# Strided attention outputs kept by residue: one ScalarE copier, a later value step and a later exponential in a fused decoder layer

## The chip, the cores and the metric

The kernel runs on one core of a Trainium2 chip. Time is device microseconds of one execution. A core has a matmul engine (TensorE, PE; its weight loads are PEld), VectorE (DVE), ScalarE (ACT), GpSimd (POOL), and SyncE (SP), which here only issues DMAs. Each engine takes its instructions in the order in which the program lists them; semaphores order the engines among themselves.

## The reference, cut to what matters

One layer of a hybrid decoder in fp32: an input projection, attention with eight heads and a gating unit beside it, an output projection and a SwiGLU network, for 2048 prompt positions and a small sample group. The change touches the prompt's attention alone. Each head evaluates three branches (window, dilation): (128, 1), (512, 4) and (2048, 16). They are merged with weights proportional to their softmax sums:

```python
    s = jnp.einsum('bnqrhc,bnkrhc->bnrhqk', qb, kc).astype(jnp.float32)
    s = s * (HEAD_DIM ** -0.5) + bias[None, None, None]
    s = jnp.where(valid[None, :, None, None], s, NEG_INF)
    lse = jax.nn.logsumexp(s, axis=-1)
    p = jnp.exp(s - lse[..., None])
    o = jnp.einsum('bnrhqk,bnkrhc->bnqrhc', p.astype(vc.dtype), vc)
...
    w = jax.nn.softmax(jnp.stack(lses, axis=0), axis=0)
    return jnp.sum(w[..., None] * jnp.stack(outs, axis=0).astype(jnp.float32), axis=0)
```

## The kernel before, in words

**Stages.** The input projection comes first (to about 610 us), then attention (about 610 to 1000 us), the output projection and the SwiGLU network in three blocks of positions.

**Items and steps.** The first two branches are computed together as a *band*: for each of 16 query blocks of 128 positions, scores against up to five key blocks. The third branch is *strided*: positions with the same residue modulo 16 form a block of 128, four residues make one strided item, so a head has 16 band items and 4 strided items. In heads 1 to 6 the order is `OTHER`: 0, 1, s, 2, 3, 4, 5, s, 6 to 9, s, 10 to 13, s, 14, 15, with s a strided item; so strided items stand at places 2, 7, 12 and 17 of the 20. The first and last heads have other orders.

A small planner, `Plan`, sets the order of the program. `at(step, phase, fn)` records a call; calls run sorted by step, then by phase (`early`, `exp`, `low`, `scores`, `turn`, `mid`, `values`, `out`, `misc`, `store`), then by when they were recorded. One item starts in each step: item i at step x = 240 + i.

- A band item has its scores (L864) at step x and its bias, with a running minimum, on VectorE (L870) at x + 1. The exponential on ScalarE (L875) is at x + 2, and the transposes on TensorE (L891) at x + 3, emptied by ScalarE (L896) and VectorE (L902). Four band items form a group. Behind its last item the group's values (L916) are computed in two parts, at x + 4 and x + 5, into PSUM bank 3, and copied out by ScalarE (L930; for a head's first group L927 and L928) at x + 6, "early".
- For a strided item GpSimd first reorders keys and queries (L937, three casts from every sixteenth position) at x - 2. The scores (L945) are at x, the bias and minimum on VectorE (L950, L952) and GpSimd (L953) at x + 1, the exponential (L956) at x + 3, its row sum (L960) and the transposes (L965, L967) at x + 4. The values (L974) go into the same PSUM bank 3, at the first step from x + 6 on that is not in the set `taken`; `strided_out` copies them out at the next step, "early".

`taken` holds the steps of the band values, so that two groups don't meet in bank 3. Scores go through two PSUM buffers in turn, so that the scores of item x need the bias of item x - 2.

**Outputs of the strided branch.** `o3` holds a head's strided outputs as [channel, i, residue], position 16 i + residue. `strided_out` writes it in two halves of two residues each, ScalarE one (L986), VectorE the other (L984); consecutive elements of one residue lie 64 bytes apart.

**Factors and merge.** When a head's items are done, `Stats` works out a weight for each branch and position: a product (L1002), two small matmuls (L1008), a copy (L1012), `weights_a` (three operations on VectorE, L1018 to L1020, and an exponential on ScalarE, L1021), `weights_b` (L1026 to L1030), and a store to DRAM (L1034). `merge_load` reads the factors back, spread over the partitions, and `merge` combines four pieces of 512 positions in three parts: band output times factor (L1055), strided output times factor (L1057), sum (L1059). GpSimd does this during the next head, one part a step from step 11 to 22, among its other work; in the last head VectorE does the first piece.

Of the kernel before, what the change touches and what calls it, by code (L numbers as in the profile page):

```python
# [10 lines left out]
F32 = mybir.dt.float32  # L11
F32R = mybir.dt.float32r
AF = mybir.ActivationFunctionType
# [6 lines left out]
P = 128  # L20
T = 2048
NT = T // P
# [3 lines left out]
C = 64  # L26
# [38 lines left out]
def hymba_step(ctx: ExitStack, tc: tile.TileContext, A: dict, O: dict):  # L65
    nc = tc.nc
    sync, act, dve, pool, pe = nc.sync, nc.scalar, nc.vector, nc.gpsimd, nc.tensor
# [7 lines left out]
    turn = [0, 0, 0, 0]  # L75
# [87 lines left out]
    rp = right.enter_context(tc.tile_pool(name="rp", bufs=1, side="right"))  # L163
# [480 lines left out]
    B0 = 240  # L644
# [49 lines left out]
    for half in range(2):  # L694
        for ki, kind in enumerate(ORDER[half]):
            for gi, tiles in enumerate(GROUPS):
# [13 lines left out]
                for j, tj in enumerate(tiles):  # L710
                    t = half * 8 + tj
                    e, ph = e0 + 2 * j, "out"
                    if last:
                        e, ph = e0, "early"
# [261 lines left out]
    def strided_out(it):  # L976
        r4, h = it["n"], it["h"]
        if r4 == 0:
            o3s[h] = rp.tile([P, P, NT], F32, name="o3", tag="wide", bufs=2)
        for z in range(2):  # L980
            dst = o3s[h][0:C, :, r4 * 4 + z * 2:r4 * 4 + z * 2 + 2].rearrange("p i r -> p r i")
            src = it["o"][z * C:(z + 1) * C, z * 256:(z + 1) * 256].rearrange("p (r i) -> p r i", r=2)
            if z:
                dve.tensor_copy(dst, src)  # L984
            else:
                act.activation(dst, src, AF.Copy)  # L986

    s12 = {}

# [2 lines left out]
    class Stats:  # L992
# [21 lines left out]
        def weights_a(self):  # L1014

            m3 = self.st["t"][0:self.r1, 2, :]
            self.f = f = self.small("f", 3)
            dve.tensor_tensor(f[:, 2, :], self.s[:, 0, :], m3, op=OP.min)  # L1018
            dve.tensor_sub(f[:, 0, :], f[:, 2, :], self.s[:, 0, :])
            dve.tensor_sub(f[:, 1, :], f[:, 2, :], m3)  # L1020
            act.activation(f[:, 0:2, :], f[:, 0:2, :], AF.Exp)  # L1021

        def weights_b(self):
            f, m = self.f, self.f[:, 2, :]
# [25 lines left out]
    def merge(h, ch, eng, part=None):  # L1050
        f1, f3 = mf[h, ch]
        x = obs[h][:, ch * 512:(ch + 1) * 512]
        y = o3s[h].rearrange("p i r -> p (i r)")[:, ch * 512:(ch + 1) * 512]
        if part in (None, 0):
            eng.tensor_mul(x, x, f1)  # L1055
        if part in (None, 1):
            eng.tensor_mul(y[0:C], y[0:C], f3[0:C])  # L1057
        if part in (None, 2):
            eng.tensor_add(x[0:C], x[0:C], y[0:C])  # L1059

    def merge_store(h, c0, c1):
        for z in range(2):
# [46 lines left out]
    for h in range(H):  # L1109
        r4 = 0  # L1110
        for n in FIRST if h == 0 else LAST if h == H - 1 else OTHER:
            if n == "s":
                items.append(dict(kind="s", h=h, n=r4))
                r4 += 1
                continue
            if n % 4 == 0:
                grp = {}
            items.append(dict(kind="b", h=h, n=n, grp=grp))
            if n % 4 == 3:

                taken.update(B0 + len(items) - 1 + y for y in (4, 5))
    NI = len(OTHER)
    L = B0 + len(items) - 1
    at(222, "misc", begin, 0)
# [13 lines left out]
    def stats_of(h, steps, r0, r1):  # L1138
        d = {}
        at(*steps[0], lambda: d.update(s=Stats(h, sts[h], r0, r1)))  # L1140
        for (y, ph), fn in zip(steps, "a b c weights_a weights_b store".split()):
            at(y, ph, lambda fn=fn: getattr(d["s"], fn)())

    for h in range(H):
# [4 lines left out]
        if end:  # L1149

            x = s0 - NI
            stats_of(h, [(x + y, ph) for y, ph in ((14, "early"), (14, "turn"), (15, "early"), (15, "misc"), (16, "early"), (16, "mid"))], 0, 64)
            steps = ((2, "early"), (2, "turn"), (3, "early"), (4, "early"), (5, "early"), (5, "early"))
            at(x + 18, "mid", merge_load, h, 0)
            at(x + 18, "mid", merge_load, h, 1)
            for part in range(3):
# [1 line left out]
                at(x + 21 + part, "store", merge, h, 1, pool, part)  # L1158
            at(x + 24, "store", merge_store, h, 0, 2)
        else:  # L1160
            steps = ((2, "misc"), (3, "misc"), (4, "early"), (4, "misc"), (5, "misc"), (6, "mid"))

            for ch, (a, b) in enumerate(((8, 11), (8, 14), (14, 17), (20, 24) if ahead else (17, 20))):
                at(s0 + a, "mid", merge_load, h, ch)
# [887 lines left out]
```

## Time and profile before

| what | value |
|---|---|
| median of 3 runs | 2718.59 us (2712.78 to 2735.36) |
| the profiled execution | 2712.56 us, span 2710.8 us |
| busy share of the span | PE 94%, PEld 80%, DVE 51%, ACT 44%, POOL 51% |
| mean granted TensorE clock | 0.962 |

The span runs from the first to the last instruction; an execution's own time is a little longer. A row of instructions in order of time has the start, the busy time, the engine, the line, the operation, output and inputs, and the number of instructions; in brackets how long the engine stood idle before it, and what ended that. A row of a group has the total and the mean duration (in ns) behind the bar, then the idle time before and its causes. A row of waits reads "engine, what it stood before <- what it waited for: us in total, times, longest".

### The profile page before, as it was taken

The page shows a single profiled execution, that of the slowest core. Times are in us where ns is not written, and L with a number is a line of the kernel's source. Part 1 is how long each engine was busy: PE and PEld are TensorE (multiplying, and loading weights), DVE is VectorE, ACT ScalarE, POOL GpSimd, SP SyncE. Part 2 cuts the span into 40 slices and gives each one's busy share as a digit, 9 for nine tenths or more (in the row PEclk, how much of TensorE's full clock was granted, in tenths as well). Part 3 has the DMA queues.
Part 4 walks back from the last instruction along what each step waited for, and adds up shares of the span by engine and source line. Part 5 has one row for each costly group of instructions (what it writes and reads, how often), then busy time and mean ns, then how long its engine had stood idle before and what let it go on. Part 6 is the DMA issues. An engine that isn't in the chain of part 4 may idle for free.

```text
span 2710.8 us, 38610 instructions
## 1 busy us (share of the span) xinstructions
PE 2539.2 (94%) x13578; PEld 2180.0 (80%) x13578; DVE 1380.8 (51%) x2756; ACT 1200.5 (44%) x2537; POOL 1388.1 (51%) x1048
## 2 busy tenths in 40 slices
PE   8998999998888778899999999999999998999997
PEld 6777777776666557899899988899999987999996
DVE  3268784436665753443444455444444456444445
ACT  6423344436565545545445444423232335433333
POOL 1035553224756752767676653535454533666663
PEclk9999999999988889799999999899999998899998
DMA  8765844674555456345555465445454453455553
GB/s 249 215 195 152 260 144 138 183 254 157 173 154 161 116 156 201 117 152 177 169 164 186 136 186 187 133 147 196 154 180 166 170 174 129 162 197 203 198 201 118
DMA packets 298166, 468.46 MB, mean 173 GB/s; under 512 B 26839, under 2 KB 163208, under 8 KB 292084
## 3 DMA queue, kind: packets, MB, share of 16 engines
q1 hardware_dynamic: 283588, 443.31, 50.7%
q10 hardware_dynamic: 14384, 22.68, 3.3%
q8 instruction: 108, 1.77, 0.3%
q14 instruction: 86, 0.70, 0.1%
HBM read 374.38 MB, written 161.64 MB: 198 GB/s over the span
## 4 chain that ended last, share of the span: by engine, by line
PE 49%; POOL 9%; issue 9%; DVE 5%; ACT 5%; DMA 4%; SPq 1%; POOLq 0%; DVEq 0%; ACTq 0%
PE ps_o L1627 11%; PE ps_m L1555 7%; PE ps_m L1554 7%; PE ps_m L1556 7%; POOL op L1497 2%; DMA ab_d<-pair 2%; PE ps_o L916 2%; PE ps_s L864 1%; ACT fr L1465 1%; PE ps_s L945 1%; POOL pair L1477 1%; POOL fr L1480 1%; POOL pair L1486 1%; PE ps_t L891 1%; POOL dw L137 1%
## 5 line engine op out<-in xcount | busy, mean ns | idle before, releaser
L1497 POOL TENSOR_TENSOR op<-fr,op 128x512 fp32r<-128x512 f32 x385 | 488.6, 1298 | 316.6 <-ACT op L1493 299.0
L1554 PE MATMUL ps_m<-xh,op 128*128 128x384 f32 (+4 forms) x1932 | 629.8, 326 | 8.5 <-ACT xh L1431 5.4
L1555 PE MATMUL ps_m<-xl,op 128*128 128x384 f32 (+4 forms) x1932 | 627.8, 325 | 7.1 <-DVE xl L1434 7.1
L1556 PE MATMUL ps_m<-xh,op 128*128 128x384 f32 (+4 forms) x1932 | 627.6, 325 | 0.0
L1627 PE MATMUL ps_o<-dw,hw 128*128 128x512 f32 x2040 | 484.3, 392 | 9.3 <-DVE acc L1629 9.3
L1627 PEld LDWEIGHTS ps_o<-dw,hw 128*128 128x128 f32 x2040 | 379.7, 188 | 91.7 <-DVE acc L1629 15.9
L1554 PEld LDWEIGHTS ps_m<-xh,op 128*128 128x128 f32 x1932 | 377.6, 195 | 13.7 <-ACT xh L1431 6.1
L1555 PEld LDWEIGHTS ps_m<-xl,op 128*128 128x128 f32 x1932 | 378.0, 196 | 11.8 <-DVE xl L1434 7.8
L1556 PEld LDWEIGHTS ps_m<-xh,op 128*128 128x128 f32 x1932 | 377.3, 195 | 0.0
L1629 DVE TENSOR_TENSOR acc<-acc,ps_o 128x512 f32<-128x512 f32 (+1 forms) x362 | 247.0, 686 | 214.1 <-PE ps_o L1627 214.1
L1594 ACT ACTIVATE ps_t<-zn 128x384 f32<-128x384 f32 (+1 forms) x126 | 58.3, 463 | 485.9 <-DVE zn L1577 376.7
L1493 ACT ACTIVATE op<-fr 128x512 fp32r<-128x512 f32 x396 | 235.6, 622 | 16.2 <-DMA fr<-ab_d 13.3
L137 POOL TENSOR_TENSOR dw<-fd,dw 128x1024 fp32r<-128x1024 f32 x66 | 158.6, 2403 | 122.6 <-ACT dw L134 122.5
L317 PE MATMUL ps_s<-wh,xh 128*128 128x512 f32 x480 | 197.4, 411 | 6.5 <-ACT xh L134 6.0
L318 PE MATMUL ps_s<-wl,xh 128*128 128x512 f32 x480 | 191.8, 400 | 1.7 <-DVE wl L225 1.7
L319 PE MATMUL ps_s<-wh,xl 128*128 128x512 f32 x480 | 191.2, 398 | 0.0
L1497 POOL TENSOR_TENSOR op<-pair,op 128x512 fp32r<-128x512 f32 x63 | 81.3, 1299 | 117.0 <-ACT op L1493 117.0
L1604 ACT ACTIVATE hw<-ps_t 128x384 fp32r<-128x384 f32 (+1 forms) x126 | 56.1, 453 | 176.7 <-DVE ps_t L1600 175.7
L317 PEld LDWEIGHTS ps_s<-wh,xh 128*128 128x128 f32 x480 | 92.5, 193 | 36.8 <-issue 8.4
L318 PEld LDWEIGHTS ps_s<-wl,xh 128*128 128x128 f32 x480 | 92.8, 193 | 20.5 <-DVE wl L225 3.2
L603 POOL TENSOR_TENSOR vl<-kv,vh 100x512 fp32r<-100x512 f32 (+1 forms) x32 | 45.5, 1424 | 124.5 <-ACT vh L597 44.4
L319 PEld LDWEIGHTS ps_s<-wh,xl 128*128 128x128 f32 x480 | 92.4, 192 | 20.4 <-DVE xl L137 0.3
(452 smaller groups left out, 4576.6 us busy)
## 6 DMA issues: line engine op xcount, KB each, us to landing
fr<-ab_d SPq DMA_DIRECT2D x308, 256.0 KB
fd<-in_w_down_dram SPq DMA_DIRECT2D x66, 512.0 KB
out_ks_dram<-in_cache_k_dram SPq DMA_DIRECT2D x56, 512.0 KB
out_vs_dram<-in_cache_v_dram SPq DMA_DIRECT2D x56, 512.0 KB
ab_d<-fr SPq DMA_DIRECT2D x88, 256.0 KB
raw<-in_w_in_dram SPq DMA_DIRECT2D x72, 256.0 KB
qk_d<-pair SPq DMA_DIRECT2D x64, 256.0 KB
ab_d<-pair SPq DMA_DIRECT2D x63, 256.0 KB
```

Source lines behind the costliest of these rows:

```text
L137: (eng_lo or pool).tensor_sub(lo, src, hi.bitcast(F32))
L317: pe.matmul(o[j], xh[:, k, :], wh, start=(k == 0), stop=False)
L318: pe.matmul(o[j], xh[:, k, :], wl, start=False, stop=False)
L319: pe.matmul(o[j], xl[:, k, :], wh, start=False, stop=(k == KD - 1))
L1493: act.activation(ops[f, j][0], ab[f][j], AF.Copy)
L1497: (pool if f or j in POOL_LOW else dve).tensor_sub(lo_, ab[f][j], hi.bitcast(F32))
L1554: pe.matmul(out, wh[:, ks], xh[:, :, k], start=(k == 0), stop=False)
L1555: pe.matmul(out, wh[:, ks], xl[:, :, k], start=False, stop=False)
L1556: pe.matmul(out, wl[:, ks], xh[:, :, k], start=False, stop=(k == 3))
L1594: act.activation(g, c, AF.Silu)
L1627: pe.matmul(ps[0:nr], l_, r_[:, cs], start=(z == 0 and y == 0), stop=(z == FC - 1 and y == len(pairs) - 1))
L1629: dve.tensor_add(B.acc[i][0:nr, cs], B.acc[i][0:nr, cs], ps[0:nr])
```

## The change

`o3` is kept as [channel, residue, i], so each residue's 128 positions are contiguous. ScalarE makes both copies of `strided_out`. The merge walks through `o3` with the residue innermost, so that neighbouring elements lie 512 bytes apart: its product with the factor reads and writes that way, its sum reads that way; band output and factors keep their order. `taken` also holds the step of the band copy, x + 6, so strided values move to a later step. The exponential leaves `weights_a`, becomes `weights_e`, and comes a step later, while the rest of `weights_a` comes earlier in its step.

```diff
         if r4 == 0:
-            o3s[h] = rp.tile([P, P, NT], F32, name="o3", tag="wide", bufs=2)
+            o3s[h] = rp.tile([P, NT, P], F32, name="o3", tag="wide", bufs=2)
         for z in range(2):
-            dst = o3s[h][0:C, :, r4 * 4 + z * 2:r4 * 4 + z * 2 + 2].rearrange("p i r -> p r i")
-            src = it["o"][z * C:(z + 1) * C, z * 256:(z + 1) * 256].rearrange("p (r i) -> p r i", r=2)
-            if z:
-                dve.tensor_copy(dst, src)
-            else:
-                act.activation(dst, src, AF.Copy)
+            act.activation(o3s[h][0:C, r4 * 4 + z * 2:r4 * 4 + z * 2 + 2, :],
+                           it["o"][z * C:(z + 1) * C, z * 256:(z + 1) * 256].rearrange("p (r i) -> p r i", r=2), AF.Copy)
...
-            act.activation(f[:, 0:2, :], f[:, 0:2, :], AF.Exp)
+
+        def weights_e(self):
+            act.activation(self.f[:, 0:2, :], self.f[:, 0:2, :], AF.Exp)
...
-        y = o3s[h].rearrange("p i r -> p (i r)")[:, ch * 512:(ch + 1) * 512]
+        y = o3s[h][0:C].rearrange("p r i -> p i r")[:, ch * 32:(ch + 1) * 32, :]
+        by_token = lambda v: v[0:C].rearrange("p (i r) -> p i r", r=NT)
...
-            eng.tensor_mul(y[0:C], y[0:C], f3[0:C])
+            eng.tensor_mul(y, y, by_token(f3))
         if part in (None, 2):
-            eng.tensor_add(x[0:C], x[0:C], y[0:C])
+            eng.tensor_add(by_token(x), by_token(x), y)
...
-                taken.update(B0 + len(items) - 1 + y for y in (4, 5))
+                taken.update(B0 + len(items) - 1 + y for y in (4, 5, 6))
...
-        for (y, ph), fn in zip(steps, "a b c weights_a weights_b store".split()):
+        for (y, ph), fn in zip(steps, "a b c weights_a weights_e weights_b store".split()):
...
-            stats_of(h, [(x + y, ph) for y, ph in ((14, "early"), (14, "turn"), (15, "early"), (15, "misc"), (16, "early"), (16, "mid"))], 0, 64)
-            steps = ((2, "early"), (2, "turn"), (3, "early"), (4, "early"), (5, "early"), (5, "early"))
+            stats_of(h, [(x + y, ph) for y, ph in ((14, "early"), (14, "turn"), (15, "early"), (15, "misc"), (16, "early"), (16, "early"), (16, "mid"))], 0, 64)
+            steps = ((2, "early"), (2, "turn"), (3, "early"), (4, "early"), (4, "early"), (5, "early"), (5, "early"))
...
-            steps = ((2, "misc"), (3, "misc"), (4, "early"), (4, "misc"), (5, "misc"), (6, "mid"))
+            steps = ((2, "misc"), (3, "misc"), (4, "early"), (4, "early"), (5, "early"), (5, "misc"), (6, "mid"))
```

How this moves instructions, at three places. On TensorE, around a strided item's values in a middle head (`ps_o` and `ps_t` are PSUM banks, `eT` the transposed exponentials, `sq` the reordered operands), the rows before were:

```order
L864 MATMUL ps_s<-k,ql 128x256
L974 MATMUL ps_o_6494<-eT,v 64x128 x4
L864 MATMUL ps_s<-k,qh 128x384
L864 MATMUL ps_s<-k,qh 128x256
L864 MATMUL ps_s<-k,ql 128x384
L864 MATMUL ps_s<-k,ql 128x256
L965 MATMUL ps_t_6515<-ident,e_6437 128x128 x4
L891 MATMUL ps_o_6522<-ident,e 128x128 x3
L891 MATMUL ps_t_6527<-ident,e 128x128 x2
L945 MATMUL ps_s<-sq 128x128 x8
```

The same place with the change:

```order
L864 MATMUL ps_s<-k,ql 128x256
L864 MATMUL ps_s<-k,qh 128x384
L864 MATMUL ps_s<-k,qh 128x256
L864 MATMUL ps_s<-k,ql 128x384
L864 MATMUL ps_s<-k,ql 128x256
L965 MATMUL ps_t_6507<-ident,e_6437 128x128 x4
L891 MATMUL ps_o_6514<-ident,e 128x128 x3
L891 MATMUL ps_t_6519<-ident,e 128x128 x2
L974 MATMUL ps_o_6522<-eT,v 64x128 x4
L945 MATMUL ps_s<-sq 128x128 x8
```

The four value matmuls went behind the next scores and transposes, and now stand right ahead of the strided scores.

On VectorE, where a head's factors are made (`s` holds the copied sums, `f` the factors, the L870 rows are band biases of the next head), the rows before were:

```order
L1012 COPY s_5874<-ps_o_5871 128x32
L870 ISA e,st<-ps_s,b 128x384
L870 ISA st 128x1
L1018 TENSOR_TENSOR f<-s_5874,st 128x16
L1019 TENSOR_TENSOR f<-f,s_5874 128x16
L1020 TENSOR_TENSOR f<-f,st 128x16
L870 ISA e,st<-ps_s,b 128x512
L870 ISA st 128x1
L1026 TENSOR_TENSOR dd<-f,s_5874 128x16
```

With the change (the lines of the file moved up by four there):

```order
L1008 COPY s_5874<-ps_o_5871 128x32
L1014 TENSOR_TENSOR f<-s_5874,st 128x16
L1015 TENSOR_TENSOR f<-f,s_5874 128x16
L1016 TENSOR_TENSOR f<-f,st 128x16
L870 ISA e,st<-ps_s,b 128x384
L870 ISA st 128x1
L870 ISA e,st<-ps_s,b 128x512
L870 ISA st 128x1
L1024 TENSOR_TENSOR dd<-f,s_5874 128x16
```

The three small operations went ahead of one band bias.

On ScalarE, behind a band group's copy (here a head's first group), the rows before were:

```order
L928 ACTIVATE ob<-ps_o_5981 64x384
L956 ACTIVATE e_5959<-e_5959 128x512
L875 ACTIVATE e,st<-e,st 128x640
L986 ACTIVATE o_6027<-ps_o_6016 64x2x128
L875 ACTIVATE e,st<-e,st 128x640
L967 ACTIVATE eT<-ps_t_6039 128x512
```

With the change:

```order
L928 ACTIVATE ob<-ps_o_5981 64x384
L956 ACTIVATE e_5959<-e_5959 128x512
L875 ACTIVATE e,st<-e,st 128x640 x2
L967 ACTIVATE eT<-ps_t_6031 128x512
L896 ACTIVATE pt<-ps_t_6038 128x3x128
L981 ACTIVATE o_6052<-ps_o_6046 64x256 x2
```

The strided copy, now two of them, went behind one band exponential and the copies of the transposes, and stands a step later.

## The prediction

> **What bounds the kernel now.** I read busy time by stretch, since the change touches only the attention stage, about 610 to 1000 us. The first row below is the whole stage, the second six whole heads of it; the columns are the busy time of PE, PEld, DVE, ACT and POOL, the granted clock, and the DMA share. The last two come from a finer cut of the same view.
>
> ```profile
> 610.00:1000.00 390.00, 324.51 (x2134) 236.22 (x2131) 249.87 (x573) 226.67 (x529) 248.64 (x227) 0.91 0.51 150
> 640.00:925.00 285.00, 240.05 (x1617) 177.79 (x1616) 178.80 (x430) 170.28 (x400) 183.56 (x171) 0.92 0.54 160
> ...
> 762.00:765.00 3.00, 1.30 (x12) 1.33 (x13) 2.61 (x7) 1.96 (x6) 1.86 (x2) 1.00 0.02 9
> 765.00:768.00 3.00, 3.00 (x15) 2.38 (x14) 2.19 (x5) 1.79 (x4) 0.73 (x1) 0.54 0.00 0
> ```
>
> In the six heads TensorE works 240 of 285 us; the 45 us in which it stands still are what this change can win, and no other engine is busy more than 65%. So the stage is a chain of waits, not a full engine. The clock adds to it: right behind a stretch in which TensorE worked 1.30 of 3 us, the granted clock is 0.54; over the six heads it averages 0.92, so another 8%, 23 us, goes to slow clock.
>
> Next the waits. The first four rows are TensorE's own in those six heads; the last two are of other engines, over the whole stage.
>
> ```profile
> PE ps_s L945 <- DVE st L870: 23.3, 17, 1.8
> PE ps_o L974 <- ACT ob L930: 10.6, 10, 1.8
> PE ps_s L945 <- POOL ob L1059: 2.9, 2, 1.5
> ...
> PE ps_o L974 <- ACT ob L928: 2.5, 6, 0.4
> ...
> DVE o L984 <- ACT o L986: 60.0, 30, 3.5
> ...
> ACT f L1021 <- DVE f L1020: 24.7, 9, 7.1
> ```
>
> TensorE waits before the strided scores (L945) for a late band bias on VectorE (L870), and before the strided values (L974) for ScalarE's copy out of the same PSUM bank (L930, L928). Behind the first stands the fifth row: VectorE's half of the strided copy (L984) waits for ScalarE's half (L986) in 30 of 32 cases, 2 us each, although the two write different elements. They interleave in one tile. Behind the second stands in part the last row, ScalarE standing before the exponential of the factors.
>
> One head is enough to see the pattern, because every later one repeats it:
>
> ```profile
> 726.25 1.08 PE L945 MATMUL ps_s<-sq 128*128 128x128 f32 x8 [1.45 <-DVE st L870]
> 735.10 0.66 PE L974 MATMUL ps_o<-eT,v 128*64 128x128 f32 x8 [0.33 <-ACT ob L930]
> 738.49 1.08 PE L945 MATMUL ps_s<-sq 128*128 128x128 f32 x8 [1.29 <-DVE st L870]
> 746.95 0.66 PE L974 MATMUL ps_o<-eT,v 128*64 128x128 f32 x8 [1.78 <-ACT ob L930]
> 750.64 1.94 PE L945 MATMUL ps_s<-sq 128*128 128x128 f32 x8 [0.66 <-DVE st L870]
> 759.45 0.66 PE L974 MATMUL ps_o<-eT,v 128*64 128x128 f32 x8 [0.42 <-ACT ob L928]
> 763.70 1.08 PE L945 MATMUL ps_s<-sq 128*128 128x128 f32 x8 [1.81 <-DVE st L870]
> ```
>
> These seven waits add to 7.74 us a head. Call the four strided groups A (726.25), B (735.10 and 738.49), C (746.95 and 750.64) and D (759.45 and 763.70). C's L945 also ran at half clock, 1.94 us where the others took 1.08.
>
> **The change, part by part.** *The copies.* VectorE loses L984, ScalarE gets a second copy, and both now write contiguous runs.
>
> ```profile
> L984 DVE COPY o<-ps_o 64x256 f32<-64x256 f32 x32 | 19.3, 603 | 60.2 <-ACT o L986 60.0
> L986 ACT ACTIVATE o<-ps_o 64x256 f32<-64x256 f32 x32 | 19.2, 600 | 2.4 <-PE ps_o L974 2.2
> ...
> L896 ACT ACTIVATE pt<-ps_t 128x256 f32<-128x256 f32 x5 | 1.9, 385 | 10.8 <-PE ps_t L891 10.8
> L902 DVE COPY pt<-ps_t 128x256 f32<-128x256 f32 x65 | 27.4, 421 | 36.3 <-PE ps_t L891 36.1
> ...
> L1057 POOL TENSOR_TENSOR o<-o,pair 64x512 f32<-64x512 f32 x26 | 33.6, 1292 | 0.0
> L1059 POOL TENSOR_TENSOR ob<-ob,o 64x512 f32<-64x512 f32 x31 | 39.7, 1280 | 1.7
> ...
> L937 POOL CAST sq<-k 128x512 fp32r<-128x512 f32 x32 | 33.8, 1058 | 7.8 <-PE ps_s L318 7.5
> L953 POOL TENSOR_TENSOR e<-e,st 128x512 f32<-128x512 f32 x32 | 33.4, 1045 | 126.0 <-DVE st L952 106.8 <-PE ps_t L891 18.3 <-PE ps_o L891 0.8
> ...
> L137 POOL TENSOR_TENSOR dw<-fd,dw 128x1024 fp32r<-128x1024 f32 x66 | 158.6, 2403 | 122.6 <-ACT dw L134 122.5
> ```
>
> A contiguous ScalarE copy of 256 columns takes 385 ns (L896) where the strided one takes 600, so two cost 0.77 us for 0.60: between 0.77 and 1.20 us, and I take 0.77. Over 32 groups that is 5.4 us more on an engine busy 60%, hidden by its idle 40%; uncovered it would be 5.4 us. VectorE is freed of 19.3 us of work and of 60 us of standing. What that gives TensorE, at A:
>
> ```profile
> 722.20 0.62 ACT L956 ACTIVATE e<-e 128x512 f32<-128x512 f32 x1
> ...
> 724.15 0.61 DVE L984 COPY o<-ps_o 64x256 f32<-64x256 f32 x1 [2.10 <-ACT o L986]
> ...
> 725.27 0.82 DVE L870 CUSTOM_DVE_ANT_0 e<-ps_s,b 128x640 f32<-128x640 f32 x1
> ```
>
> Without L984, the row sum behind it (0.65 us) can start when the exponential ends, 722.82; the bias then ends about 1.7 us earlier, at 724.4. TensorE was ready at 726.25 - 1.45 = 724.8. So VectorE's part of the wait goes entirely, at A as at B and D.
>
> *The strided values one step later.* L974 no longer follows right behind the band group's values and so no longer meets the band copy (L930, L928), which now has a step of over 2 us. At B and D that removes 0.33 and 0.42 us. Its 0.66 us of matmul stay before the same L945. The next user of the bank comes a step and a half later, while the two copies need 0.77 us; covered, and one stall of about 0.8 us if not.
>
> *What is late next: GpSimd.* L945 also needs the reordered operands (L937, three casts), and in A and B these stand among the merges in GpSimd's queue.
>
> ```profile
> 718.66 1.04 POOL L953 TENSOR_TENSOR e<-e,st 128x512 f32<-128x512 f32 x1 [4.25 <-DVE st L952]
> ...
> 724.14 1.08 POOL L937 CAST sq<-ql 128x512 fp32r<-128x512 f32 x1
> ...
> 729.94 1.04 POOL L953 TENSOR_TENSOR e<-e,st 128x512 f32<-128x512 f32 x1 [0.91 <-DVE st L952]
> ...
> 735.50 1.08 POOL L937 CAST sq<-ql 128x512 fp32r<-128x512 f32 x1
> ...
> 742.09 1.04 POOL L953 TENSOR_TENSOR e<-e,st 128x512 f32<-128x512 f32 x1 [1.60 <-DVE st L952]
> ```
>
> The casts for A end at 725.22, 0.4 us after TensorE would be ready: with some latency 0.5 us of A's 1.45 stay, even at old merge times. For B they end at 736.58, 0.6 us before TensorE (737.20), and 0.3 us after B's first wait is gone too. Now the merges read and write the strided tile. Let L1057 grow by a, and L1059 by b. One L1059 stands between L953 and the casts of A: A keeps 0.5 + b. Behind A two merges of each kind delay the casts of B: B keeps 2a + 2b - 0.3, not below 0. GpSimd has 0.91 and 1.60 us of idle time to pay from in these two stretches, which is what these slacks say. In C and D it idles for microseconds.
>
> The trace has no such merge, so a and b are bounded. Below: 0, since the number of elements and operands is the same. Above: each strided operand costs a whole extra pass like L937's 1.06 us; L1057 has two (read and write), L1059 one, so a = 2.1, b = 1.06. (Near its middle lies L137, twice the elements for 2.40, or +1.1.) I take 0.25 for both, near the lower end: the nearest row that steps through memory on GpSimd is L937, at 64 bytes, and its 1058 ns equal the 1045 of L953, which streams one operand contiguously; the engine's own pace, 2.0 ns an element, seems to hide the step. I don't take 0, because ScalarE pays 215 ns for 256 strided writes and VectorE 603 - 421 = 182, some 0.8 ns an element.
>
> The Trainium skill speaks against the change here: "GPSIMD Engine Reference", section "Performance pitfalls for Q7 kernels", puts reads that step over more than 8 bytes at half again the cost per element. L937 steps 64 bytes and does not show it against L953, though no contiguous cast is there to compare. By it the sum would be that of rival 1, 2696.
>
> *The factors.* The three small VectorE operations (L1018 to L1020) move ahead of a band bias, and the exponential a step later.
>
> ```profile
> 742.95 0.55 DVE L870 CUSTOM_DVE_ANT_0 e<-ps_s,b 128x384 f32<-128x384 f32 x1
> 743.42 0.74 DVE L1018 TENSOR_TENSOR f<-s,st 128x16 f32<-128x16 f32 x1
> ...
> 744.31 0.56 PE L864 MATMUL ps_s<-k,qh 128*128 128x384 f32 x2
> ...
> 745.10 1.05 DVE L1020 TENSOR_TENSOR f<-f,st 128x16 f32<-128x16 f32 x1
> ...
> L1027 DVE TENSOR_TENSOR dd<-f,st 128x16 f32<-128x16 f32 x8 | 1.3, 162 | 0.0
> ```
>
> They run from 743.42 to 746.15, 2.73 us for 16 columns, each about as long as a GpSimd operation (L937, 1.06) of those that run beside them. Now that bias (L870 at 742.95) queues behind them: from about 743.0 come 2.73 and its own 0.55, so it ends near 746.3, and the scores that reuse its bank (L864, 744.31) start 2.0 us later. So C trades its wait of 1.78 for one of 2.0 in front of L864; only the path behind gets shorter, and I find L945 at 750.0 to 750.5 instead of 750.64. C keeps 2.0 of 2.44 us. If GpSimd stood idle there, these operations would cost what L1027 costs, 0.16 us each, and C's waits would go; if a longer GpSimd operation met them, C would lose instead.
>
> *The sum.* Per head 7.74 - 2.0 (C) - 0.75 (A) - 0.7 (B) = 4.3 us. Six whole heads, and the first and last together as one more (the stage has 65.5 us of standing TensorE, 20.5 of it outside the six heads, and I count a fifth of that): 7 x 4.3 = 30 us. Clock: of the 23 us a quarter, 6, because the slow spells behind D's waits (the rows from 762 us) should go, those behind C's not. Lost again: the last head's merges stand in the chain to the output projection, with about four strided operations, 1 us, and VectorE does one of them; I put 2. So 30 + 6 - 2 = **34 us off the profiled 2712.56 (span 2710.8), 2679 us**. That execution is 6 us under the median of 2718.59, at the bottom of the runs; a median of after may lie a few us higher.
>
> On the clock, the Trainium skill's "TensorE: Matmul & The Clock Gate", "What's actually happening", says a gate halves TensorE's clock after a window of low activity and releases it after a busy one; the 0.54 behind the stretch with 1.30 us of work agrees. By it alone, all 23 us could come back if every wait went; I keep 6.
>
> **The rivals.** (1) *Merges half again as long* (1.29 to 1.93, a = b = 0.64): each read or write that steps costs GpSimd some 1.2 ns an element more, about what ScalarE's rows show. A keeps 1.14, B 2.26: 2.34 a head, 16 in all, plus 3 of clock, less 3 at the end: 2696. For it: the penalty on two other engines. Against: L937. The Trainium skill's rule above would give this case. (2) *The merges become the bound*: at a = 2.1, b = 1.06, A keeps 1.56 and B 6.06, with C 9.6 against 7.74 before: 13 us lost over the stage and 6 at the end, 2732. It decides from a = b = 1.14, merges of 2.4 us, where the sum per head is zero. Against it: no GpSimd row steps up like that. (3) *The waits move and nothing is won*: VectorE, free, is followed by ScalarE, whose copies now stand in front of a band exponential and wait for L974 in its queue. ScalarE idles 40%, which speaks against it; only L974's 0.33 and 0.42 would stay won, 5 us in all, 2707.
>
> **How the numbers follow.** Forecast 0.58 (its own range 2660 to 2692), rival 1 0.22, rival 2 0.08, rival 3 0.12. Low end: a = b = 0, C's waits gone too, twice the clock: 7 x 7.2 + 12 - 2 = 60 off, 2653; I put 2655. High end: rival 2, 2730. One per cent, 27 us, is about what a measurement of this kernel tells from no change. Faster by more: four fifths of the forecast and a little of rival 1, 0.50. Slower by more than 1% needs even longer merges than rival 2: 0.06. Between: 0.44.
>
> **What would show it.** L984 gone and ScalarE's copies near 385 ns; L945's waits for L870 nearly gone from 23.3 us, and replaced at A and B by the casts; L974's waits for the band copy gone; a wait of about 2 us before L864 once a head; the strided merges at 1.5 us, and the mean clock of the stage above 0.92. Merges above 1.9 us make the prediction wrong on the slow side; waits at C that vanish make it wrong on the fast side.

## The result and the profile after

The changed kernel takes **2691.61 us** (median of 10 runs, 2681.43 to 2699.31), against 2712.44 us for the kernel before in the same comparison (10 runs). The ratio is 0.9923, 95% interval 0.9903 to 0.9943: 21 us faster, where 34 were forecast. The profiled execution took 2691.25 us.

The page's head and the two windows of before, of the kernel after. The last row is a third window, six heads' worth of work, from one strided item to the same one six heads on; the columns are the stretch, its length, the busy time of PE, PEld, DVE, ACT and POOL, the granted clock, the DMA share and GB/s.

```profile
span 2689.5 us, 38648 instructions
...
PE 2533.0 (94%) x13578; PEld 2170.3 (81%) x13578; DVE 1375.7 (51%) x2724; ACT 1206.2 (45%) x2569; POOL 1408.6 (52%) x1048
```

```profile
610.00:1000.00 390.00, 334.10 (x2178) 236.74 (x2177) 255.27 (x555) 236.54 (x567) 275.33 (x233) 0.94 0.57 165
640.00:925.00 285.00, 248.82 (x1694) 176.92 (x1690) 186.26 (x429) 181.72 (x445) 214.60 (x185) 0.96 0.56 166
...
630.36:896.25 265.89, 236.27 (x1624) 167.55 (x1622) 174.17 (x409) 174.49 (x427) 192.59 (x167) 0.97 0.57 170
```

The same six heads in the kernel before:

```profile
632.36:917.03 284.67, 239.66 (x1621) 177.63 (x1621) 180.30 (x433) 170.62 (x401) 181.55 (x168) 0.93 0.53 159
```

The matmuls are the same (x1621 and x1624; a few records are missing). So the stretches can be subtracted: 284.67 - 265.89 = 18.8 us won. Of these, 3.4 us are shorter matmuls (239.66 to 236.27, the clock at 0.97 for 0.93), and 15.4 us are less standing (45.0 to 29.6).

For all later comparisons I use one number of each profile, the **strided stage**: from the start of the first strided score matmul (L945) to that of the last. It is read from the one line of the view on L945, here before and after:

```profile
L945 PE MATMUL ps_s<-sq x256: 272/276/455, 612.3 to 947.6; 128*128 128x128 f32 x128
```

```profile
L945 PE MATMUL ps_s<-sq x256: 272/276/466, 611.4 to 925.9; 128*128 128x128 f32 x128
```

335.3 us became 314.5: 20.8 less, while the spans differ by 21.3. Between these two executions, all but 0.5 us of the difference lies in this stage; the rest of the span is 2375.5 and 2375.0 us.

What TensorE waits for now, over the stage (total, times, longest):

```profile
PE ps_s L864 <- DVE st L870: 16.7, 13, 3.9
PE ps_s L945 <- POOL sq L937: 13.2, 20, 2.1
...
PE ps_t L965 <- ACT e L956: 3.2, 9, 1.3
PE ps_t L891 <- ACT e L875: 3.0, 12, 1.3
...
PE ps_o L965 <- ACT e L956: 1.7, 3, 1.3
...
PE ps_s L945 <- DVE st L870: 0.7, 1, 0.7
```

The old first wait, 23.3 us before L945 for the bias, is down to 0.7, and the waits for the band copy before L974 are gone. In their place stand the band scores (L864) behind a late bias and the strided scores behind GpSimd's casts (L937). One head of it, TensorE's rows with a wait:

```profile
719.19 1.00 PE L945 MATMUL ps_s<-sq 128*128 128x128 f32 x7 [0.15 <-POOL sq L937]
726.23 0.36 PE L864 MATMUL ps_s<-k,qh 128*128 128x256 f32 x1 [0.18 <-DVE st L870]
726.90 0.66 PE L965 MATMUL ps_t<-ident,e 128*128 128x128 f32 x4 [0.19 <-ACT e L956]
727.71 0.55 PE L891 MATMUL ps_o<-ident,e 128*128 128x128 f32 x3 [0.15 <-ACT e L875]
729.81 0.33 PE L945 MATMUL ps_s<-sq 128*128 128x128 f32 x1 [0.75 <-POOL sq L937]
730.80 1.00 PE L945 MATMUL ps_s<-sq 128*128 128x128 f32 x7 [0.67 <-POOL sq L937]
738.88 0.56 PE L864 MATMUL ps_s<-k,qh 128*128 128x384 f32 x2 [2.26 <-DVE st L870]
751.66 0.66 PE L965 MATMUL ps_o<-ident,e 128*128 128x128 f32 x4 [1.26 <-ACT e L956]
```

With two of 0.15 us behind (L891), this head waits 5.9 us; the next one 4.1, with 1.61 at L864 and without the 1.26. The forecast was 7.74 - 4.3 = 3.4.

The groups behind these waits, on GpSimd and on ScalarE (busy time, mean ns of one):

```profile
L1058 POOL TENSOR_TENSOR ob<-ob,o 64x512 f32<-64x512 f32 x31 | 48.8, 1576 | 1.7
L1056 POOL TENSOR_TENSOR o<-o,pair 64x512 f32<-64x512 f32 x26 | 41.8, 1607 | 0.0
...
L981 ACT ACTIVATE o<-ps_o 64x256 f32<-64x256 f32 x64 | 24.1, 377 | 3.6 <-PE ps_o L974 3.1
```

### The profile page after: what moved, and what is told of

It is laid out like the page before. It is cut to its first block, busy times and chain, and to the rows that moved or that the text cites. A ratio compares the mean times of both kernels' runs of the same rounds, so it can differ in the third digit from the quotient of the medians.

```text
span 2689.5 us, 38648 instructions
## 1 busy us (share of the span) xinstructions
PE 2533.0 (94%) x13578; PEld 2170.3 (81%) x13578; DVE 1375.7 (51%) x2724; ACT 1206.2 (45%) x2569; POOL 1408.6 (52%) x1048
## 5 line engine op out<-in xcount | busy, mean ns | idle before, releaser
L1492 ACT ACTIVATE op<-fr 128x512 fp32r<-128x512 f32 x396 | 235.8, 622 | 21.1 <-DMA fr<-ab_d 17.7
```

The source lines that it names most:

```text
L1492: act.activation(ops[f, j][0], ab[f][j], AF.Copy)
```

## The experiments

The ratio is to the kernel before, timed beside each on the same chip. Its interval is 0.2 to 0.5% (5 to 15 us) to either side, too wide for a difference of a few us between two kernels. The stage shows those, but is one reading from one profiled execution. In these executions the rest of the span differs more than many of the stages do (2367 to 2389 us), so that medians and stages do not rank all kernels alike.

The stage holds the same 1874 or 1875 matmuls in every kernel. The third column is the time in it in which TensorE stands: the length less the busy time that the view of windows gives for it. What is left, 268 to 290 us, is the time that the matmuls themselves took. Only standing can be put down to waits. The clock has a part in the rest (0.92 granted in the stage before, 0.96 after), but why the matmuls took longer in one kernel than in another was not followed.

| kernel | strided stage, us | TensorE stands in it, us | median, us | ratio, 95% interval |
|---|---|---|---|---|
| before | 335.3 | 55.6 | 2712.44 to 2714.24, in five comparisons | 1 |
| after (the change) | 314.5 | 38.9 | 2691.61 | 0.9923 [0.9903, 0.9943] |
| copies alone | 314.4 | 40.3 | 2687.79 | 0.9911 [0.9880, 0.9942] |
| step alone | 336.5 | 46.5 | 2705.68 | 0.9973 [0.9953, 0.9994] |
| factors alone | 329.5 | 55.6 | 2706.48 | 0.9970 [0.9950, 0.9990] |
| after, merges in runs | 309.1 | 35.8 | 2681.03 | 0.9891 [0.9856, 0.9926] |
| after, factors back behind the bias | 314.3 | 33.4 | 2689.03 | 0.9893 [0.9853, 0.9933] |
| after, old layout | 307.3 | 32.7 | 2685.03 | 0.9894 [0.9856, 0.9933] |
| after, two copiers | 317.2 | 44.0 | 2693.31 | 0.9916 [0.9885, 0.9947] |
| after, last merge later | 338.2 | 53.2 | 2719.92 | 1.0024 [1.0001, 1.0046] |
| before, ScalarE alone | 307.9 | 38.2 | 2689.12 | 0.9906 [0.9868, 0.9943] |
| after, factors from PSUM | 307.4 | 35.0 | 2682.67 | 0.9879 [0.9841, 0.9917] |
| after, old layout, factors from PSUM | 296.8 | 24.1 | 2673.13 | 0.9851 [0.9818, 0.9885] |
| before, ScalarE alone, factors from PSUM | 299.9 | 32.2 | 2675.37 | 0.9855 [0.9801, 0.9909] |

### Which part brings the gain

**Copies alone**: before, with the new layout, both copies on ScalarE and the merge that follows from it.

```diff
-            o3s[h] = rp.tile([P, P, NT], F32, name="o3", tag="wide", bufs=2)
+            o3s[h] = rp.tile([P, NT, P], F32, name="o3", tag="wide", bufs=2)
...
-            if z:
-                dve.tensor_copy(dst, src)
-            else:
-                act.activation(dst, src, AF.Copy)
+            act.activation(o3s[h][0:C, r4 * 4 + z * 2:r4 * 4 + z * 2 + 2, :],
...
-            eng.tensor_mul(y[0:C], y[0:C], f3[0:C])
+            eng.tensor_mul(y, y, by_token(f3))
...
```

> Of the change only the layout by residue, ScalarE's two copies and the merge that walks with steps; the value step and the factors as before. Theory (VectorE's stand behind ScalarE's copy is the larger part): VectorE's 60 us of standing and L945's 23 us of waits for the bias are gone, GpSimd's casts keep about 1.5 us a head at the same place, L974's waits for the band copy (2.5 us a head) stay; some 3 us a head are won, 2690 to 2700 us. Rival (the value step is what wins): the waits before L974 grow, because two copies now stand in ScalarE's queue, and at most 8 us are won, above 2704 us.

**Step alone**: before, with the values one step later.

```diff
-                taken.update(B0 + len(items) - 1 + y for y in (4, 5))
+                taken.update(B0 + len(items) - 1 + y for y in (4, 5, 6))
```

> Of the change only the value step (the set of taken steps has x + 6 too); copies, layout and factors as before. Theory: L974's waits for the band copy (13 us in six heads) go, but VectorE still stands behind ScalarE's copy, one step later and so one step nearer to the bias that L945 needs, so those 23 us stay or grow; 2700 to 2712 us. Rival (the value step is what wins): about as fast as the whole change, 2692 us.

**Factors alone**: before, with the three small operations ahead of the bias and the exponential as a call of its own one step later.

```diff
-            steps = ((2, "misc"), (3, "misc"), (4, "early"), (4, "misc"), (5, "misc"), (6, "mid"))
+            steps = ((2, "misc"), (3, "misc"), (4, "early"), (4, "early"), (5, "early"), (5, "misc"), (6, "mid"))
...
```

> Of the change only the factors: the three small operations earlier in their step, the exponential a step later. Theory: one wait is traded for another; L974's 1.78 us a head behind the exponential goes, and about 2 us before L864 come, since a band bias queues behind the small operations: 2709 to 2716 us. Rival (ScalarE's stand before the exponential was a cost of its own): 1.8 us a head are won, 2696 to 2700 us.

The copies alone have the whole gain (stage 314.4, the change 314.5), with a median 2 us below the range that was expected. With the step alone the stage is 1.2 us longer, not shorter: TensorE stands 9.1 us less, and its matmuls take 10.3 us more (290.0 for 279.7). Its time, 0.3% less, is within its expected range. The factors alone win 5.8 us of stage, all of it in shorter matmuls (274.0 for 279.7), and none in standing; their median of 2706.48 lies between the ranges of the two cases. In the step's waits one sees what stays, and what comes new:

```profile
DVE o L984 <- ACT o L986: 51.9, 30, 4.4
PE ps_s L864 <- DVE st L870: 32.6, 33, 3.5
...
PE ps_t L891 <- ACT e L875: 2.4, 13, 0.5
...
PE ps_t L965 <- ACT e L956: 2.1, 9, 0.3
...
PE ps_o L965 <- ACT e L956: 1.4, 3, 1.0
```

VectorE still stands 52 us behind ScalarE's copy; the stand is only later in the program, and now makes the bias late for a band score instead of a strided one. The last three rows are waits for ScalarE's exponentials, which the kernel before and the copies alone hardly have (0.2 us before L891 in each, none before L965).

### Are the merges what is missing?

**After, merges in runs**: the stepped reads and writes of the merge go over contiguous memory instead. It leaves the arithmetic's amount as it is, but pairs strided outputs with the factors of other positions.

```diff
-        y = o3s[h][0:C].rearrange("p r i -> p i r")[:, ch * 32:(ch + 1) * 32, :]
-        by_token = lambda v: v[0:C].rearrange("p (i r) -> p i r", r=NT)
+        y = o3s[h][0:C].rearrange("p r i -> p (r i)")[:, ch * 512:(ch + 1) * 512]
...
-            eng.tensor_mul(y, y, by_token(f3))
+            eng.tensor_mul(y, y, f3[0:C])
...
```

> The changed kernel, but the merge takes the strided outputs in the order in which they lie, in contiguous runs (so positions are combined with the wrong factors; the amount of work is the same). It prices the stepping merges. Theory (GpSimd is full between two strided groups of each head, so its longer merges are on the path): the merges fall from 1.6 to 1.28 us, L945's waits for the casts from 13 us to under 5, and the time by about 10 us, to 2679 to 2685 us. Rival (the longer merges are covered): waits and time as with the change, 2691 us.

**After, old layout**: ScalarE makes both copies, but into the old interleaved tile; the merges are the old ones.

```diff
...
+            dst = o3s[h][0:C, :, r4 * 4 + z * 2:r4 * 4 + z * 2 + 2].rearrange("p i r -> p r i")
+            src = it["o"][z * C:(z + 1) * C, z * 256:(z + 1) * 256].rearrange("p (r i) -> p r i", r=2)
+            act.activation(dst, src, AF.Copy)
...
```

> The changed kernel with the layout of before: ScalarE makes both copies, but writes with steps of 64 bytes (two of 0.6 us for two of 0.38), and the merges run through contiguous memory (1.28 us). Theory (GpSimd is on the path, ScalarE is not): 14 us more work on ScalarE cost little and GpSimd's shorter merges win what the contiguous ones of the other run win; 2680 to 2688 us, faster than the change. Rival (ScalarE's queue is on the path, as the waits for its exponentials suggest): slower than the change, 2695 us or more.

The waits with merges in runs, and then those with the old layout:

```profile
PE ps_s L864 <- DVE st L870: 20.9, 13, 3.0
PE ps_s L945 <- POOL sq L937: 6.0, 10, 1.4
```

```profile
PE ps_s L864 <- DVE st L870: 18.3, 13, 2.7
PE ps_s L945 <- POOL sq L937: 3.7, 5, 1.4
```

The wait for the casts halves or more (13.2 to 6.0 and 3.7), the one for the bias grows by a part of that (16.7 to 20.9 and 18.3), and the stage falls by 5.4 and 7.2 us (standing by 3.1 and 6.2). So stepping costs the change 5 to 7 us of stage, in GpSimd's merges. ScalarE's strided copies, 607 ns for 377, cost TensorE nothing that shows.

**After, last merge later**: the last quarter's merge moves from steps 20 to 22 into 23 to 25, and its store three steps, to clear the stretch between A and B.

```diff
-            for ch, (a, b) in enumerate(((8, 11), (8, 14), (14, 17), (20, 24) if ahead else (17, 20))):
+            for ch, (a, b) in enumerate(((8, 11), (8, 14), (14, 17), (20, 24) if ahead else (17, 23))):
...
```

> The changed kernel, but the last quarter of each merge of heads 0 to 5 comes three steps later, where GpSimd idles (the store follows). Theory (GpSimd is full between the strided groups and idle for 7 us behind them): B's waits of 1.4 us a head before L945 go, GpSimd's idle time shrinks there, and 6 to 9 us are won: 2682 to 2686 us. Rival (the casts of the next group, or the factors' small operations that run beside GpSimd, become late instead): no gain, 2691 us or more.

It lost 23.7 us of stage against the change: TensorE stands 14.3 us more, and its matmuls take 9.4 us more. One head shows how. The merges now run beside the factors' small operations, and one of those, 16 columns wide, takes 3.53 us. VectorE's bias behind it is late, and the scores wait 5.20:

```profile
744.77 3.53 DVE L1014 TENSOR_TENSOR f<-s,st 128x16 f32<-128x16 f32 x1
...
751.28 0.90 PE L864 MATMUL ps_s<-k,qh 128*128 128x384 f32 x2 [5.20 <-DVE st L870]
```

Over the stage the waits for the bias grow by 12 us against the change (24.3 for 16.7 before L864, 5.3 for 0.7 before L945). The rest of the loss was not followed.

### What makes VectorE stand, and the factors' order

**After, two copiers**: VectorE makes the second copy again, in the new layout, so that the two halves no longer interleave.

```diff
...
+            dst = o3s[h][0:C, r4 * 4 + z * 2:r4 * 4 + z * 2 + 2, :]
...
+            if z:
+                dve.tensor_copy(dst, src)
+            else:
+                act.activation(dst, src, AF.Copy)
```

> The changed kernel with the layout by residue, but VectorE makes the second copy again; the two halves no longer interleave. Theory (the stand of VectorE behind ScalarE came from the interleaving, not from the copy): no wait between the copies, VectorE has 0.42 us more and ScalarE 0.38 us less a group, and the time stays within 5 us of the change, 2687 to 2697 us. Rival (VectorE's own work was the cost, or it waits all the same): the waits of L945 or L864 for the bias come back, 2700 us or more.

The time came out as expected and its reason did not:

```profile
DVE o L984 <- ACT o L986: 39.6, 28, 4.9
PE ps_s L864 <- DVE st L870: 22.4, 25, 3.6
```

VectorE waits for ScalarE's half in 28 of 32 cases although each half is a block of its own. Interleaving is not what orders them. They still write one tile and read one PSUM bank. One tile alone does not order two writers, as a pair of copies of the kernel before shows: L896 and L902 empty the transposes of one band item out of two banks into interleaved places of one tile, `pt`, and overlap in time:

```profile
720.67 0.49 ACT L896 ACTIVATE pt<-ps_o 128x384 f32<-128x384 f32 x1 [2.44 <-PE ps_o L891]
720.89 0.42 DVE L902 COPY pt<-ps_t 128x256 f32<-128x256 f32 x1 [1.31 <-PE ps_t L891]
```

That leaves the common bank as the likely cause; it was not tried by itself.

The stage is 2.7 us longer than with one copier (TensorE stands 5.1 more). So 18.1 of the 20.8 us are won here with VectorE still standing 39.6 us: with short copies, later values and the later exponential, its stand costs little. Whether the later values and exponential together would do this in the old layout too was not run.

**After, factors back behind the bias**: the three small operations at their old place.

```diff
-            steps = ((2, "misc"), (3, "misc"), (4, "early"), (4, "early"), (5, "early"), (5, "misc"), (6, "mid"))
+            steps = ((2, "misc"), (3, "misc"), (4, "early"), (4, "misc"), (5, "early"), (5, "misc"), (6, "mid"))
```

> The changed kernel, but in heads 1 to 6 and their like the three small operations stand again behind the band bias of their step; the exponential stays a step later. Theory (C's wait before L864 comes from the bias that queues behind them): that wait, 1.6 to 2.3 us a head, goes, L974 no longer stands right behind the band copy, and 8 to 14 us are won on the changed kernel: 2678 to 2684 us. Rival (the wait only moves to the next bias, which then queues behind them): within 3 us of the changed kernel, 2691 us.

Stage 314.3 for 314.5: whether they stand ahead of one bias or the next, some score waits for a bias behind them (13.7 us before L864 for 16.7). TensorE stands 5.5 us less (33.4 for 38.9), and its matmuls take 5.3 more, in the slowest of this kernel's four executions (2705.05 us); so these runs do not tell whether the order is worth a few us. What makes the operations long is still there.

### The two losses taken out

**Before, ScalarE alone**: one edit to the kernel before.

```diff
-            if z:
-                dve.tensor_copy(dst, src)
-            else:
-                act.activation(dst, src, AF.Copy)
+            act.activation(dst, src, AF.Copy)
```

> The kernel before with one edit: ScalarE makes both strided copies, into the old interleaved layout, so that VectorE has no copy left there; the strided values, the factors and the merges stay as they were. Theory: the whole gain is VectorE freed of its stand behind ScalarE's copy, and the layout only costs merges; then the strided stage of the profile (first to last strided scores) lasts 306 to 312 us against 335.3 before and 314.5 for the change, and the kernel 2680 to 2688 us. Rival: the merges were not what the change lost, and the step and the factors had to be there for it; then the stage stays at 314 to 320 us and the kernel at 2688 to 2695.

**After, factors from PSUM**: the sums are taken where the matmul left them (`p`), into another part of the bank (`q`); min(d, 0) of both differences gives the same two exponents. No operation of the three has two operands in SBUF.

```diff
-            dve.tensor_tensor(f[:, 2, :], self.s[:, 0, :], m3, op=OP.min)
-            dve.tensor_sub(f[:, 0, :], f[:, 2, :], self.s[:, 0, :])
-            dve.tensor_sub(f[:, 1, :], f[:, 2, :], m3)
+            p, q = self.p[0:self.r1, 0:NT], self.p[0:self.r1, 2 * NT:4 * NT]
+            dve.tensor_sub(q[:, 0:NT], m3, p)
+            dve.tensor_sub(q[:, NT:2 * NT], p, m3)
+            dve.tensor_scalar(f[:, 0:2, :], q.rearrange("p (a t) -> p a t", a=2), 0.0, None, op0=OP.min)
```

> The changed kernel with one edit: the three small VectorE operations of the factors (about 0.7 to 1.1 us each beside a GpSimd operation) take their sums out of PSUM, where the matmul left them, and no operation of the three reads two operands from SBUF. Theory: they last as long as the GpSimd operation beside them because both read two operands from SBUF; then each lasts 0.1 to 0.3 us, the wait of 1.6 to 2.3 us before the scores behind them goes, and of 14.5 us of such waits in the stage 10 or more come back: stage 302 to 306 us, kernel 2679 to 2683. Rival: they are late for another reason (the matmul or the copy ahead of them), or the wait is taken over by the exponential next in line; then the stage stays at 312 to 316 and the kernel at 2689 to 2693.

**After, old layout, factors from PSUM**: the two edits together.

> The version that both findings point to: the old interleaved layout with both copies by ScalarE, strided values and exponential one step later as in the change, and the factors' small operations on PSUM operands. If the merges (7 us of stage) and the small operations (10 us) are separate losses, the stage lasts 295 to 299 us and the kernel 2668 to 2676 us, faster than the changed kernel by 0.6 to 0.9%. Rival: both losses sit in the same wait, and the second brings nothing more; then 305 to 308 us of stage and 2682 to 2686.

**Before, ScalarE alone, factors from PSUM**: the same without the later step and exponential.

> The kernel before with two edits: ScalarE makes both strided copies (old layout), and the factors' three small VectorE operations work on PSUM operands; the strided values and the exponential stay at their old steps. It differs from the version with all four pieces (stage 296.8 us, 2673 us) only by that one step. Theory: with the two large losses gone the step is worth something after all, because the strided values again stand behind ScalarE's band copy (16 to 20 us of such waits in the version with the copies alone, part of them by the late exponential); then the stage lasts 302 to 308 us and the kernel 2678 to 2686. Rival: the step is worth nothing here either, the waits only stand in another place; then 295 to 299 us and 2669 to 2677.

ScalarE alone gives a stage of 307.9, as its theory had it, though its median of 2689.12 is 1 us above the expected range and inside the rival's. One edit does at least what the whole change does, by its stage 6.6 us more, of which 0.8 is standing and the rest shorter matmuls (269.8 for 275.6). It keeps waits that the change removes, and pays for them no more than the change pays elsewhere:

```profile
PE ps_o L974 <- ACT ob L930: 16.0, 12, 2.5
PE ps_s L945 <- POOL sq L937: 10.6, 17, 1.4
PE ps_o L974 <- ACT ob L928: 3.9, 7, 1.0
PE ps_s L864 <- DVE st L870: 3.7, 3, 2.3
```

With the factors from PSUM, the wait before L864 goes from 16.7 to 3.9, as that theory had it, but part of it is taken over by L945 (13.2 + 0.7 before the edit, 15.2 + 7.7 behind it):

```profile
PE ps_s L945 <- POOL sq L937: 15.2, 19, 2.1
...
PE ps_s L945 <- DVE st L870: 7.7, 6, 1.9
...
PE ps_s L864 <- DVE st L870: 3.9, 7, 2.6
```

So the stage falls by 7.1 us, to 307.4, where 302 to 306 was expected: theory and rival each hold in part. Together with the old layout it falls by 17.7, to 296.8, more than the sum of the single steps (7.2 and 7.1); standing falls by 14.8, for 6.2 and 3.9. By these readings, one of each, each was hiding part of the other. The last pair tells what the step and the later exponential are worth once both losses are out: 299.9 without, 296.8 with, 3 us, too little for the medians to tell (2675.37, 2673.13). TensorE stands 8.1 us less with them, and its matmuls take 5.0 more. Without them the stage lies between that expectation's two cases, 0.9 us above its rival's, and the median is the rival's.

The version with both edits is the fastest: 2673.13 us, and its interval, 0.9818 to 0.9885, lies wholly below that of the change. Why the operands matter is plain in a stretch of this version, VectorE above and GpSimd below:

```profile
734.01 0.18 DVE L1016 TENSOR_TENSOR ps_t<-st,ps_t 128x16 f32<-128x16 f32 x1
734.23 0.18 DVE L1017 TENSOR_TENSOR ps_t<-ps_t,st 128x16 f32<-128x16 f32 x1
734.45 0.19 DVE L1018 TENSOR_SCALAR f<-ps_t 128x32 f32<-128x32 f32 x1
...
735.64 1.66 DVE L1026 TENSOR_TENSOR dd<-f,s 128x16 f32<-128x16 f32 x1
737.22 0.17 DVE L1027 TENSOR_TENSOR dd<-f,st 128x16 f32<-128x16 f32 x1
...
734.13 1.05 POOL L937 CAST sq<-k 128x512 fp32r<-128x512 f32 x1
735.13 1.10 POOL L937 CAST sq<-qh 128x512 fp32r<-128x512 f32 x1
736.16 1.10 POOL L937 CAST sq<-ql 128x512 fp32r<-128x512 f32 x1
```

All these VectorE operations have 16 or 32 columns. Beside the same casts, those with an operand in PSUM take 0.18 or 0.19 us. The one with both operands in SBUF takes 1.66, through the rest of one cast and all of the next, to within 0.04 us of its end (737.30 and 737.26); the one behind it, with GpSimd done, takes 0.17.

## Why the prediction was right or wrong

**Direction and place: right.** What bounded the stage was waits, and the largest, VectorE standing behind ScalarE's copy, is the one whose removal brings the gain: the copies alone have 20.9 us of stage, for 20.8 of the whole change, and ScalarE's two copies in the old layout 27.4. It is not the only way to it, as the two copiers show, who keep most of that stand and 18.1 us of the gain; why it costs so little there stays open.

**The size: 21 us for 34.** Over six heads, standing fell by 15.4 us where 6 x 4.3 = 26 were counted, and the clock gave 3.4 where six sevenths of 6, 5.1, were. The clock's term was near; the waits' term was 10 us too large. The median lies 0.4 us inside the range given for the forecast's own case (2660 to 2692) and 4 us from rival 1's 2696; its spread, 2681.43 to 2699.31, does not tell the two apart. The sizes of the merges do, below. In the head at 719 us, by the prediction's own terms:

| term | forecast left | measured left |
|---|---|---|
| A | 0.75 | 0.15 |
| B | 0.7 | 0.75 + 0.67 = 1.42 |
| C, before L864 | 2.0 | 2.26 (1.61 in the next head) |
| D | 0 | 0 |
| behind C, before L965 (exponential) | not in the sum | 1.26 (0.27 in the next head) |
| 0.15 to 0.19 us before L864, L965, L891 | not in the sum | 0.82 |

- **Copies**: contiguous copies at 377 ns for a forecast 385, and hidden. Right. The reason given for VectorE's stand, interleaved halves, is refuted by the two copiers; the sum did not need it.
- **The merges, a and b**: 1.607 - 1.292 = 0.315 and 1.576 - 1.280 = 0.296 for a forecast of 0.25. Nearly right, and what was said to happen happened: B's wait is now the casts. But B kept 1.4 us where 2a + 2b - 0.3 gives 0.9 at the measured sizes, and A 0.15 where 0.5 + b gives 0.8. The -0.3 counts what B's own first wait gives back, and not that TensorE comes to B earlier by what A gave back, while GpSimd can't follow: from 712.27 to 739.29 us its rows follow one another without a gap above 0.1 us. So the split between A and B was wrong, and their sum right: 1.57 for 1.45. The forecast charged the longer merges 7 x (0.25 + 0.7) = 6.7 us, and the two kernels with short ones are 5.4 and 7.2 us of stage faster. Over the six heads the casts keep TensorE waiting 7.7 us (6 x 1.45 = 8.7 forecast); with merges in runs 1.6 there, with the old layout nothing.
- **C**: the forecast that it would trade its wait for one before L864 was right: 2.26 in three of the six heads, 1.61 in the other three, for 2.0.
- **The exponentials are what the sum lacks.** Over the six heads TensorE waits 4.9 us for L956 before L965 and 2.3 for L875 before L891, 1.2 us a head, most of it in pieces of 0.15 to 0.3; twice it is 1.3 (at 751.66 and 840.48 us). The step alone has such waits, the copies alone hardly: they come with the later values. TensorE, which stood before L974 for ScalarE's band copy, now comes earlier to the transposes, and in the head above the exponential stands behind that same copy in ScalarE's queue: L927 and L928 at 749.87 and 750.47, L956 from 750.98 to 751.61, L965 at 751.66. So the 0.33 and 0.42 us that the sum takes as gone come back a few instructions later, nearly to the digit: 0.19 + 0.15 at 726.90 and 727.71, and 0.27 + 0.16 at 795.34 and 796.15 in the next head. The prediction looked for exponentials behind the strided copies (rival 3), set ScalarE's 40% of idle time against it, and put nothing in the sum.
- **The remainder**: 0.9 us over the six heads are small waits before L864, and some 2 us are in other places. The head at 726 us, from which all was counted, stands 7.74 us where the mean of the six is 7.5.
- **The step and the factors** were counted as part of the sum (0.33, 0.42, and C's share). On top of the copies, both together take 1.4 us of standing (40.3 to 38.9) and nothing from the stage (314.4, 314.5). The sum took each wait as separate, yet what one of them gives back, the next takes.

Rival 1 had 2696, nearer to the measured time than to its own reason: its merges, half again as long there, were 23 to 24% longer. The Trainium skill, "GPSIMD Engine Reference", "Performance pitfalls for Q7 kernels", which stood behind it, names half again for such reads; this trace shows about half of that, for an operation that has one contiguous read beside the stepped one. Rival 2 is out by these sizes. (By its own formula it keeps 6.02 us at B, not 6.06, and the sum is zero at 1.11, not 1.14; nothing hangs on either.) Rival 3, that waits only move, is nearest to what the step alone did: its largest wait moved from L945 to L864, and its stage did not get shorter.

**The signs that were named** all came: L984 gone, L945's wait for the bias at 0.7, about 2 us before L864 once a head, merges at 1.6, and a clock of 0.94 over the stage's window for 0.91 before (0.96 over the six heads'). They were right as signs, and none of them measured how much of the gain would be taken back between them.

## What to carry to other kernels

Where one engine's copy stands behind another's, give both to the one with room before anything else is rearranged: that edit alone had the whole gain here, and the layout that came with it cost 5 to 7 us of the stage. When a chain of waits bounds a stage, don't add up the waits as if each could go alone: walk the new order once through, with every engine's new arrival time, since an engine that is full between two of them (here GpSimd) pays the second from the first, and a queue that made one instruction wait (here ScalarE's) can make the next one wait too. Small VectorE operations beside a busy GpSimd are worth a look at their operands: with one of them in PSUM they kept their 0.2 us, while moving them in the order left the stage as it was.

## What the runs showed of the hardware

- A VectorE operation of 16 columns with both operands in SBUF took 0.74 to 3.53 us beside GpSimd's work in the rows shown, and 0.18 or 0.19 us with one in PSUM beside the same kind of casts (two of these three operations also write to PSUM). The Trainium skill, "SBUF — State Buffer", "Who interferes with whom", says that a VectorE instruction with two SBUF inputs contends with a GpSimd one that reads SBUF, and that the later of the two waits until the first has ended. The row of 1.66 us agrees; that the wait may run on over a second GpSimd operation, as it did there, these rows add.
- GpSimd's 64x512 product and sum took 1.61 and 1.58 us with stepped operands, 1.29 and 1.28 without. The product steps in a read and in its result, the sum in one read alone, and both grew by 0.3 us: the stepped result seems to cost nothing.
- ScalarE's copy of 64x256 out of PSUM took 600 to 607 ns into every sixteenth element and 377 ns into runs.
